# Attention on one core: a full-height second score product, and all key blocks of a unit transposed in one run

## The chip, the cores and the metric

The kernel runs on one core of a Trainium2 chip. Time is device time in microseconds (us) of one execution. Engines are TensorE (PE in the profile, with its weight loads as PEld), VectorE (DVE), ScalarE (ACT), GpSimd (POOL) and SyncE (SP, which issues most transfers). The kernel before takes 1494.95 us, the median of three runs (1494.87 to 1495.86).

## The reference

One post-norm layer of an encoder: 512 tokens, 1024 channels, all in float32. A hybrid mixer (attention in a window and a short gated convolution, both gated and projected) is followed by 16 experts, each of which takes its 64 best tokens. The change touches the attention, which is:

```python
def one_block(args):
    q_blk, n = args
    start = n * BLOCK                       # BLOCK 128, KSPAN 384
    k_blk = lax.dynamic_slice_in_dim(kp, start, KSPAN, axis=1)
    v_blk = lax.dynamic_slice_in_dim(vp, start, KSPAN, axis=1)
    ...
    s = jnp.einsum('bqgrd,bkgd->bgrqk', q_blk, k_blk) + bias
    s = jnp.where(valid, s, NEG_INF)
    m = jnp.maximum(s.max(-1), sink)
    p = jnp.exp(s - m[..., None])
    denom = p.sum(-1) + jnp.exp(sink - m)
    return jnp.einsum('bgrqk,bkgd->bqgrd', p / denom[..., None], v_blk)
```

There are 16 heads of 64 channels in 4 groups (`g`) with one key and value head each, and 4 blocks of 128 queries (`n`). A block of queries sees its own block of keys and its neighbours: three blocks, or two at the ends of the sequence.

## The kernel before

**The mixer's stream.** The mixer's projections are cut into blocks of 128 output columns (`add_blocks`: keys `k`, values `v`, queries `q`, then `c`, `x`, `b` of the convolution, then the gates and output projections). Float32 accuracy comes from splitting both operands into a rounded first part and a rest, in a 32-bit format that TensorE takes in one pass: first x first, first x rest, rest x first, so 3 products of 128x512 for each of 8 slices of the channels. `split_block` makes the parts of the weights: a cast on ScalarE (L165) and a subtraction on VectorE (L166), two blocks ahead. The generator `stream` issues the products (L181); one step of it is one slice, so three products. `F(n)` takes n steps.

**The attention is woven into this stream.** A `Unit` is one group of heads and one block of queries: 4 heads, 2 or 3 key blocks (`w` is 256 or 384 columns). For each unit the code issues 15 steps of the stream and between them the unit's scores for two heads (`scores(0)`), two heads more (`scores(1)`), exponentials (`exps`), the division by the sums (`norms`), and of the unit before it the transposes of the probabilities (`turn`) and the products with the values (`values`). What VectorE, ScalarE and GpSimd do in which order is set by a scheduler that follows program order, with freedom for what is not pinned (`pin`); TensorE keeps the order written here.

**Scores.** `k_done` and `q_done` keep the operands so that one product on 128 rows gives two of the three parts: the keys' first part `kh` lies on both halves of the partitions, and so does the keys' rest `kl`; the queries `qp` hold the first part in one half and the rest in the other. The first product (L480) multiplies the stacked query with `kh` on 128 rows. The second (L481) multiplies the half with the query's first part with `kl` on the same 64 rows. Both add up in one PSUM bank. VectorE then adds the bias and takes the maximum (L484); ScalarE takes the exponentials (L493).

**Transposes and values.** `turn(j)` transposes key block j for 4 heads (L508) into one bank, and ScalarE (j = 0, 2; L513) or VectorE (j = 1; L511) copies it to SBUF. `values` (L520) multiplies it with the values. Scores, transposes and values share a ring of five PSUM banks (`pst`), the stream has three of its own (`mmt`).

**Behind the mixer** the experts' weights (1 MB a load, issued by SP, L603) go through a ring of buffers that the mixer's operands held before; then gate, up and down products of eight pairs of experts follow.

Of the kernel before, what the change touches and what calls it, by code (L numbers as in the profile page):

```python
# [39 lines left out]
def encoder_layer(ctx: ExitStack, tc: tile.TileContext, x, ln0r, ln0c, w_in, conv_w, sink, w_ao, w_co, w_out,  # L40
# [35 lines left out]

# [1 line left out]
    xt = [xpool.tile([P, 2, D], F32, tag=f"X{i}", name=f"x{i}") for i in range(2)]  # L78
# [34 lines left out]
    class Pair:  # L113
        """An operand [P, KT, S] in its two parts, each in two tiles."""

# [14 lines left out]

# [1 line left out]
    loads = []  # L132
# [38 lines left out]
    def stream():  # L171
        opened = {}

        def product(i, k, a, b):
            nm, opnd = blocks[i][2], blocks[i][3]
            if i not in opened:
                opened[i] = ws0.pop(0), mmt(f"p_{nm}")
            ws, ps = opened[i]
            ends = k == KT - 1 and (b if i == 0 else a) == 1
            put = pin if i < 2 else lambda x: x  # L180
            put(nc.tensor.matmul(ps, ws[:, a, k, :], (opnd.lo if b else opnd.hi)(k), start=(k + a + b == 0), stop=ends))  # L181

        def order(i, k):
            """The products of a step: block, index, weight's part, operand's part. Those of the first two blocks fill
            each other's gaps, as their operands are still being made."""
            if i == 0:
                before = [(0, k - 1, 0, 1)] if k else []
                after = [(0, k, 0, 1)] if k == KT - 1 else []
                return [(0, k, 0, 0), (0, k, 1, 0), (1, k, 0, 0)] + before + after
            return ([] if i == 1 else [(i, k, 0, 0)]) + [(i, k, 0, 1), (i, k, 1, 0)]  # L190

        for i, (li, c, nm, opnd, done) in enumerate(blocks):
            for k in range(KT):
                for h in hooks.get((nm, k), ()):
                    h()
                for step in order(i, k):
                    product(*step)
                if k == KT - 1 and i + 2 < len(blocks):
                    ws0.append(split_block(i + 2))
                tick()  # L200
                yield
            done(c, opened.pop(i)[1])
# [10 lines left out]

    # position bias with the window's mask, and the values, by group of heads
    slopes = (2.0 ** (-8.0 * np.arange(1, NH + 1) / NH)).astype(np.float32)
# [10 lines left out]

    # keys: first parts and rests, each on both halves of the partitions; queries: of a head in the upper half of its
    # block the rest lies above the first part, otherwise below
    kh, kl = slot("M0", [NG, S], "kh", F32R), slot("M1", [NG, S], "kl", F32R)
# [103 lines left out]

# [1 line left out]
    src, nm, _ = loads[0]  # L335
# [25 lines left out]
    def root(t):  # L361
        """(var + EPS) ** -0.5 but for the last step, and what that step needs."""
        r, v, a, mean, var = parts0(t)
        pin(nc.scalar.activation(ln[:, t:t + 1], var, AF.Ln, bias=eps))
        pin(nc.scalar.activation(r, ln[:, t:t + 1], AF.Exp, scale=-0.5))
        pin(nc.vector.tensor_scalar(v, var, EPS, -0.5, op0=OP.add, op1=OP.mult))
# [93 lines left out]
    pin(nc.vector.tensor_scalar(sinkb[:, 1, :], sinkb[:, 0, :], -1.0, None, op0=OP.mult))  # L460
# [1 line left out]
    class Unit:  # L462
# [11 lines left out]
        def scores(self, h2):  # L474
            g, w = self.g, self.w
            pss = [pst(f"s_{self.nm}_{i}") for i in range(2)]
            keys = slice(self.b0 * P, self.b1 * P)
            for half in range(2):
                q, hs, ps = qp[g][:, 2 * h2 + half, self.qs], HALVES[half], pss[half][:, :w]
                nc.tensor.matmul(ps, q, kh[:, g, keys], start=True, stop=False)  # L480
                nc.tensor.matmul(ps, q[hs], kl[hs, g, keys], start=False, stop=True)  # L481
            for half in range(2):
                i = 2 * h2 + half
                nc.vector.tensor_tensor_reduce(self.pr[:, i, :w], pss[half][:, :w], bias[g][:, i, self.off:self.off + w],  # L484
                                               1.0, -3.0e38, OP.add, OP.max, self.mx[:, i:i + 1])
# [16 lines left out]

        def turn(self, j):
            if j >= self.b1 - self.b0:
                return
            ps = pst(f"pt_{self.nm}_{j}")
            for i in range(4):
                nc.tensor.transpose(ps[:, i * P:(i + 1) * P], self.pr[:, i, j * P:(j + 1) * P], ident)  # L508
            dst = self.pT[:, j].rearrange("p a b q -> p (a b q)")
            if j == 1:  # L510
                nc.vector.tensor_copy(dst, ps)  # L511
            else:
                nc.scalar.copy(dst, ps)  # L513

# [23 lines left out]
    for g in range(NG):  # L538
        for n in range(NT):
            u = Unit(g, n)  # L540
            u.scores(0)
            F(2)
            u.scores(1)
            F(1)
            u.exps()
            F(1)
            if prev:
                prev.turn(0)
            F(1)
            if prev:  # L550
                prev.turn(1)
            F(1)
            if prev:
                prev.turn(2)
            F(2)
            u.norms()
            F(1)
            if prev:
                prev.values()
            F(6)  # L560
            prev = u
    prev.turn(0)
    F(1)
    prev.turn(1)
    F(1)
    prev.turn(2)
    F(2)
    prev.values()

# [1 line left out]
    wo = {}  # L571
# [64 lines left out]

# [1 line left out]
    aff = const.tile([P, NT, NE], F32, name="aff")  # L638
    # candidates for the largest CAP of each column in two groups of rows: the best of the first two blocks of tokens
    # and most of the third above, the others below; the first two blocks, in two groups; and what is above and at the  # L640
    # bound, behind three empty blocks
    GROUPS, HELD = (slice(0, NE), slice(32, 32 + NE)), CAP // 2 + P
# [13 lines left out]
    def awake(a, n):  # L656
        """Keeps the tensor engine's clock up between products that wait for each other."""
        pin(nc.tensor.matmul(pst("awake")[:a.shape[1], :n], a, xt[0][:, :n], start=True, stop=True))
# [22 lines left out]
    def norm1(t):  # L681
        """Mean and (var + EPS) ** -0.5 of a block, the latter but for the last step; the logits' first part, negated."""
        m, v, l, r = (tinyt(n, f"n1_{a}{t}") for n, a in ((2, "m"), (1, "v"), (1, "l"), (3, "r")))
        st, n = stats[t]
        pin(nc.vector.bn_aggr(m, st[:, :n]))
        pin(nc.scalar.activation(l, m[:, 1:2], AF.Ln, bias=eps))
        pin(nc.scalar.activation(r[:, 0:1], l, AF.Exp, scale=-0.5))
        pin(nc.vector.tensor_scalar(v, m[:, 1:2], EPS, -0.5, op0=OP.add, op1=OP.mult))
        a = tinyt(NE, f"lga{t}")
        pin(nc.vector.scalar_tensor_tensor(a, rc[:, 0, :], m[:, 0:1], lgs[t], op0=OP.mult, op1=OP.subtract))  # L690
        norms1[t] = m, v, r, a
# [45 lines left out]
    def best(src, dst, between=lambda a: None):  # L737
        """The largest CAP of each row of src, in order, into dst; src is used up."""
        for i in range(CAP // 8):
            o = dst[:, 8 * i:8 * i + 8]  # L740
            yield pin(nc.vector.max(o, src))
            if i + 1 < CAP // 8:
                yield pin(nc.vector.match_replace(src, o, src, -1.0))
            between(top[:, 8 * i + 1:8 * i + 9])
# [88 lines left out]

# [1 line left out]
    for i, _ in enumerate(best(cand[:32 + NE], top[:32 + NE, 1:], lambda a: awake(a, 256))):  # L835
# [62 lines left out]
    def spread(ln):  # L898
        """A norm's scale and shift from the first partition to all."""
        def go(i):  # L900
# [19 lines left out]
    def affine():  # L920
        """The scale and shift of the norm, left out so far."""
        for t in range(NT):
# [91 lines left out]

# [1 line left out]
    for t in range(NT):  # L1016
# [88 lines left out]
```

## Time and profile before

| | |
|---|---|
| median of 3 runs without a profile | 1494.95 us |
| span of the profiled execution | 1493.5 us |
| TensorE busy | 1408.8 us, 94% |
| VectorE busy | 402.6 us, 27% |
| ScalarE busy | 292.1 us, 20% |
| share of the chain that ended last: TensorE | 53% |
| share of that chain: transfers | 43% |
| DMA over the span | 451.13 MB, mean 302 GB/s |

The profile comes from one execution of its own; only its span is known, not a time by the clock of the runs. The attention fills the stretch from 55.5 us (first score product) to 308 us (last product with values). Shares over the whole span mix stages with different limits, so what matters for an edit in the attention is read from this stretch. A matmul's recorded duration contains its way through the array and overlaps the next one's; the step from start to start is what a product costs while TensorE has work.

### The profile page before, as it was taken

The page shows a single profiled execution, that of the slowest core. Times are in us where ns is not written, and L with a number is a line of the kernel's source. Part 1 is how long each engine was busy: PE and PEld are TensorE (multiplying, and loading weights), DVE is VectorE, ACT ScalarE, POOL GpSimd, SP SyncE. Part 2 cuts the span into 40 slices and gives each one's busy share as a digit, 9 for nine tenths or more (in the row PEclk, how much of TensorE's full clock was granted, in tenths as well). Part 3 has the DMA queues.
Part 4 walks back from the last instruction along what each step waited for, and adds up shares of the span by engine and source line. Part 5 has one row for each costly group of instructions (what it writes and reads, how often), then busy time and mean ns, then how long its engine had stood idle before and what let it go on. Part 6 is the DMA issues. An engine that isn't in the chain of part 4 may idle for free.

```text
span 1493.5 us, 18062 instructions
## 1 busy us (share of the span) xinstructions
PE 1408.8 (94%) x7559; PEld 808.9 (54%) x7559; DVE 402.6 (27%) x892; ACT 292.1 (20%) x580; POOL 62.1 (4%) x46
## 2 busy tenths in 40 slices
PE   7999999999999999999999998998899799899985
PEld 6777777778888853453553542442452263264243
DVE  8566556653335350010010110010011010011015
ACT  5553444532223221100000000000000000000110
POOL 3000000060000001300000000000000000000001
PEclk9999999999999999999999999999999999999998
DMA  4211113232325969999999999999999999999993
GB/s 150 102 62 57 57 64 106 86 113 85 113 85 198 409 246 356 415 419 419 419 419 420 419 420 419 420 419 420 420 419 420 420 419 418 419 420 419 420 419 155
DMA packets 67205, 451.13 MB, mean 302 GB/s; under 512 B 7730, under 2 KB 10418, under 8 KB 13234
## 3 DMA queue, kind: packets, MB, share of 16 engines
q1 hardware_dynamic: 65824, 446.28, 73.9%
q10 hardware_dynamic: 1300, 3.70, 0.7%
q8 instruction: 59, 0.97, 0.3%
q14 instruction: 22, 0.18, 0.0%
HBM read 447.86 MB, written 2.10 MB: 301 GB/s over the span
## 4 chain that ended last, share of the span: by engine, by line
PE 53%; DMA 43%; DVE 3%; ACT 1%; issue 0%; SPq 0%; DVEq 0%
DMA w<-in_w_gate 25%; DMA w_d<-in_w_down 13%; PE d L983 6%; PE pu L943 4%; PE pg L943 4%; DMA w<-in_w_up 4%; PE p_x L181 3%; PE p_c L181 3%; PE p_b L181 3%; PE p_q L181 3%; PE p_ga L181 3%; PE p_co L181 3%; PE p_ao L181 3%; PE p_gc L181 3%; PE g L879 2%; PE sc L1000 2%
## 5 line engine op out<-in xcount | busy, mean ns | idle before, releaser
L943 PE MATMUL pg<-w,px 128*64 128x512 f32 x1024 | 245.1, 599 | 32.7 <-DMA w<-in_w_gate 32.4
L943 PE MATMUL pu<-w,px 128*64 128x512 f32 x1024 | 246.9, 603 | 16.5 <-DMA w<-in_w_up 16.5
L983 PE MATMUL d<-w_d,hT 128*64 128x256 f32 x2048 | 236.9, 383 | 6.6 <-DMA w_d<-in_w_down 6.5
L983 PEld LDWEIGHTS d<-w_d,hT 128*64 128x64 f32 x2048 | 142.6, 137 | 93.0 <-issue 19.2
L943 PEld LDWEIGHTS pg<-w,px 128*64 128x64 f32 x1024 | 69.0, 136 | 192.8 <-issue 102.2
L943 PEld LDWEIGHTS pu<-w,px 128*64 128x64 f32 x1024 | 64.6, 136 | 146.9 <-issue 96.0
L1005 DVE TENSOR_TENSOR acc<-acc,sc 128x256 f32<-128x256 f32 x108 | 45.5, 421 | 329.0 <-PE sc L1000 328.5
L958 DVE TENSOR_TENSOR h<-h,pu 128x512 f32<-128x512 f32 x32 | 22.0, 687 | 346.2 <-PE pu L943 346.2
L957 ACT ACTIVATE h<-pg 128x512 f32<-128x512 f32 x32 | 19.1, 597 | 331.9 <-PE pg L943 331.9
L1000 PE MATMUL sc<-ye,px 128*128 128x256 f32 x248 | 73.8, 411 | 0.0
L879 PEld LDWEIGHTS g<-px,xn 128*128 128x128 f32 x512 | 59.0, 192 | 20.5 <-issue 17.8
L992 ACT COPY ye<-d 128x256 f32<-128x256 f32 x32 | 11.9, 373 | 275.1 <-PE d L983 275.1
L1000 PEld LDWEIGHTS sc<-ye,px 128*128 128x128 f32 x248 | 40.8, 188 | 43.7 <-issue 41.2
L879 PE MATMUL g<-px,xn 128*128 128x128 f32 x512 | 63.8, 280 | 0.2 <-DVE px L871 0.2
L181 PE MATMUL p_c<-yh,ws_c 128*128 128x512 f32 x128 | 46.6, 411 | 0.0
L181 PE MATMUL p_x<-yh,ws_x 128*128 128x512 f32 x128 | 46.5, 411 | 0.0
L181 PE MATMUL p_b<-yh,ws_b 128*128 128x512 f32 x128 | 46.1, 410 | 0.0
L181 PE MATMUL p_q<-yh,ws_q 128*128 128x512 f32 x128 | 43.6, 403 | 0.0
L493 ACT ACTIVATE pr<-pr,neg 128x256 f32<-128x256 f32 (+1 forms) x64 | 35.2, 552 | 35.1 <-DVE neg L489 24.4
L181 PE MATMUL p_ga<-yh,ws_ga 128*128 128x512 f32 x128 | 40.9, 392 | 0.0
L484 DVE CUSTOM_DVE_ANT_0 pr<-s,bv 128x256 f32<-128x256 f32 (+1 forms) x64 | 31.0, 489 | 33.9 <-PE s L481 33.7
L181 PE MATMUL p_gc<-yh,ws_gc 128*128 128x512 f32 x128 | 40.1, 389 | 0.0
(264 smaller groups left out, 1646.0 us busy)
## 6 DMA issues: line engine op xcount, KB each, us to landing
w<-in_w_gate SPq DMA_DIRECT2D x128, 1024.0 KB, 19.9
w<-in_w_up SPq DMA_DIRECT2D x128, 1024.0 KB, 19.9
w_d<-in_w_down SPq DMA_DIRECT2D x127, 1024.0 KB, 19.9
raw_q<-in_w_in SPq DMA_DIRECT2D x4, 1024.0 KB, 4.8
raw_c<-in_w_in SPq DMA_DIRECT2D x4, 1024.0 KB, 4.8
raw_x<-in_w_in SPq DMA_DIRECT2D x4, 1024.0 KB, 4.9
raw_b<-in_w_in SPq DMA_DIRECT2D x4, 1024.0 KB, 4.8
raw_ga<-in_w_in SPq DMA_DIRECT2D x4, 1024.0 KB, 4.8
```

The source lines that it names most:

```text
L181: put(nc.tensor.matmul(ps, ws[:, a, k, :], (opnd.lo if b else opnd.hi)(k), start=(k + a + b == 0), stop=ends))
L484: nc.vector.tensor_tensor_reduce(self.pr[:, i, :w], pss[half][:, :w], bias[g][:, i, self.off:self.off + w], 1.0, -3.0e38, OP.add, OP.max, ...
L493: nc.scalar.activation(p, p, AF.Exp, bias=self.neg[:, i:i + 1], accum_out=self.su[:, i:i + 1])
L879: pin(nc.tensor.matmul(ps[:, i * P:(i + 1) * P], xt[t][:, (k + i) * P:(k + i + 1) * P], oh1[:, t].rearrange("p a c -> p (a c)"), start=(t ...
L943: pin(nc.tensor.matmul(pss[i][hs, :], xe[:, kk, hs], wt[:, a, k, :], start=(kk == 0), stop=(kk == KT - 1)))
L957: nc.scalar.activation(hb, pss[0], AF.Silu)
L958: nc.vector.tensor_tensor(hb, hb, pss[1], OP.mult)
L983: pin(nc.tensor.matmul(pd[hs, :256], hTs[p][:, f, hs], wt[:, a, ft, :], start=(f == 0), stop=(f == 15)))
L992: nc.scalar.copy(ye, pd[:, :256])
L1000: pin(nc.tensor.matmul(ps[:, :256], ohT[:, t * P:(t + 1) * P], ye, start=True, stop=True))
L1005: nc.vector.tensor_tensor(a, a, ps[:, :256], OP.add)
```

## The change

Two edits, and comments that were taken out (so that lines behind L480 have other numbers in the changed kernel).

1. The second score product takes the whole stacked query and `kl` on all 128 rows. It so adds rest x rest, which was left out before. Both products have the same form.
2. `turn` transposes all key blocks of a unit in one run, into two or three banks, pinned in that order, and then issues the copies. The steps of the stream that lay between the blocks are put around the run; a unit still has 15 steps, and from the second group of scores to the values there are seven as before.

```diff
@@ scores
             for half in range(2):
-                q, hs, ps = qp[g][:, 2 * h2 + half, self.qs], HALVES[half], pss[half][:, :w]
-                nc.tensor.matmul(ps, q, kh[:, g, keys], start=True, stop=False)
-                nc.tensor.matmul(ps, q[hs], kl[hs, g, keys], start=False, stop=True)
+                q, ps = qp[g][:, 2 * h2 + half, self.qs], pss[half][:, :w]
+                for i, k in enumerate((kh, kl)):
+                    nc.tensor.matmul(ps, q, k[:, g, keys], start=(i == 0), stop=(i == 1))
@@ turn
-        def turn(self, j):
-            if j >= self.b1 - self.b0:
-                return
-            ps = pst(f"pt_{self.nm}_{j}")
-            for i in range(4):
-                nc.tensor.transpose(ps[:, i * P:(i + 1) * P], self.pr[:, i, j * P:(j + 1) * P], ident)
-            dst = self.pT[:, j].rearrange("p a b q -> p (a b q)")
-            if j == 1:
-                nc.vector.tensor_copy(dst, ps)
-            else:
-                nc.scalar.copy(dst, ps)
+        def turn(self):
+
+            pss = [pst(f"pt_{self.nm}_{j}") for j in range(self.b1 - self.b0)]
+            for j, ps in enumerate(pss):
+                for i in range(4):
+                    pin(nc.tensor.transpose(ps[:, i * P:(i + 1) * P], self.pr[:, i, j * P:(j + 1) * P], ident))
+            for j, ps in enumerate(pss):
+                dst = self.pT[:, j].rearrange("p a b q -> p (a b q)")
+                if j == 1:
+                    nc.vector.tensor_copy(dst, ps)
+                else:
+                    nc.scalar.copy(dst, ps)
@@ the loop over units
             u.scores(1)
-            F(1)
+            F(2)
             u.exps()
-            F(1)
             if prev:
-                prev.turn(0)
-            F(1)
-            if prev:
-                prev.turn(1)
-            F(1)
-            if prev:
-                prev.turn(2)
+                prev.turn()
+            F(3)
+            u.norms()
             F(2)
-            u.norms()
-            F(1)
             if prev:
                 prev.values()
             F(6)
             prev = u
-    prev.turn(0)
-    F(1)
-    prev.turn(1)
-    F(1)
-    prev.turn(2)
-    F(2)
+    prev.turn()
+    F(4)
     prev.values()
```

TensorE's order where unit 0_1 (group 0, query block 1) is transposed, while unit 0_2 has its scores: `pt_0_1_j` is the bank of key block j, `p_q3_0` a block of the mixer's queries. Before:

```order
L508 MATMUL pt_0_1_0_816<-ident_98,pr_0_1_654 128x128 x4
L181 MATMUL p_q3_0_791<-yh0_278,ws_q3_0_720 128x512
L181 MATMUL p_q3_0_791<-yl0_280,ws_q3_0_720 128x512
L181 MATMUL p_q3_0_791<-yh0_278,ws_q3_0_720 128x512
L508 MATMUL pt_0_1_1_825<-ident_98,pr_0_1_654 128x128 x4
L181 MATMUL p_q3_0_791<-yh1_294,ws_q3_0_720 128x512
L181 MATMUL p_q3_0_791<-yl1_296,ws_q3_0_720 128x512
L181 MATMUL p_q3_0_791<-yh1_294,ws_q3_0_720 128x512
L508 MATMUL pt_0_1_2_834<-ident_98,pr_0_1_654 128x128 x4
```

The same place in the changed kernel:

```order
L508 MATMUL pt_0_1_0_816<-ident_98,pr_0_1_654 128x128 x4
L508 MATMUL pt_0_1_1_817<-ident_98,pr_0_1_654 128x128 x4
L508 MATMUL pt_0_1_2_818<-ident_98,pr_0_1_654 128x128 x4
L181 MATMUL p_q3_0_791<-yh0_278,ws_q3_0_726 128x512
L181 MATMUL p_q3_0_791<-yl0_280,ws_q3_0_726 128x512
L181 MATMUL p_q3_0_791<-yh0_278,ws_q3_0_726 128x512
```

The second and third block's transposes stand one and two steps of the stream earlier.

ScalarE's order at that place, as a difference: `pT_0_1` is the transposed copy of unit 0_1, `pr_0_2` the scores and exponentials of unit 0_2, `q2` and `q3` queries, `ws` parts of weights.

```order
-L513 COPY pT_0_1_655<-pt_0_1_0_816 128x512
+L514 COPY pT_0_1_655<-pt_0_1_0_816 128x512
 L260 ACTIVATE q2_143<-p_q2_1_733 64x512
+L514 COPY pT_0_1_655<-pt_0_1_2_818 128x512
 L493 ACTIVATE pr_0_2_769,su_0_2_766<-pr_0_2_769,neg_0_2_765 128x384 x4
 L494 ACTIVATE es_0_2_767<-es_0_2_767 128x4
-L513 COPY pT_0_1_655<-pt_0_1_2_834 128x512
 L165 CAST ws_c0_0_855<-raw_c0_647 128x1024
```

The third block's copy has moved from behind the four exponentials to ahead of them. In the units 1_0 to 1_3 and 3_0 to 3_3 the copies stand behind the exponentials in both kernels.

VectorE's order at that place, as a difference: `neg_0_2` is the negated maximum that the exponentials read, `es_0_2` the sink's part.

```order
+L512 COPY pT_0_1_655<-pt_0_1_1_817 128x512
+L261 SCALAR_TENSOR_TENSOR q2_143<-p_q2_1_733,q2_143 64x512
 L489 SCALAR_TENSOR_TENSOR neg_0_2_765<-mx_0_2_764,sinkb_94 128x4
 L490 TENSOR_TENSOR es_0_2_767<-sinkb_94,neg_0_2_765 128x4
-L261 SCALAR_TENSOR_TENSOR q2_143<-p_q2_1_733,q2_143 64x512
-L511 COPY pT_0_1_655<-pt_0_1_1_825 128x512
 L497 TENSOR_TENSOR rd_0_2_768<-su_0_2_766,es_0_2_767 128x4
```

The copy of the second block and a query's rest have moved ahead of the negated maximum.

## Rows read from the trace of the kernel before

**Rows 1.** The page: its header, and the granted TensorE clock in 40 slices.
```profile
span 1493.5 us, 18062 instructions
...
PEclk9999999999999999999999999999999999999998
```

**Rows 2.** The chain that ended last: start us, us, engine, what.
```profile
776.50 1.89 PE pu L943 x8
778.41 21.43 DMA w<-in_w_gate
```

**Rows 3.** Windows, the attention: busy us (x instructions) of PE, PEld, DVE, ACT, POOL.
```profile
55.50:308.00 252.50, 252.50 (x1176) 182.29 (x1176) 149.66 (x371) 112.46 (x256) 2.76 (x2) 1.00 0.22 76
```

**Rows 4.** Waits of SP's queue, 400 to 700 us: total, times, longest.
```profile
SPq L603 <- PE pu L943: 53.3, 24, 5.9
```

**Rows 5.** Line L481: duration ns min/median/max, first and last start, forms.
```profile
L481 PE MATMUL s<-kl,q x64: 378/408/439, 55.8 to 291.3; 64*128 64x256 f32 x32, 64*128 64x384 f32 x32
```

**Rows 6.** PE in order of time, two groups of scores: start us, us, what.
```profile
115.89 0.28 PE L480 MATMUL s<-kh,q 128*128 128x256 f32 x1
116.10 0.38 PE L481 MATMUL s<-kl,q 64*128 64x256 f32 x1
116.41 0.38 PE L480 MATMUL s<-kh,q 128*128 128x256 f32 x1
...
117.04 0.50 PE L181 MATMUL p_c<-yh,ws_c 128*128 128x512 f32 x1
117.37 0.39 PE L181 MATMUL p_c<-yl,ws_c 128*128 128x512 f32 x1
117.60 0.63 PE L181 MATMUL p_c<-yh,ws_c 128*128 128x512 f32 x2
...
130.88 0.33 PE L480 MATMUL s<-kh,q 128*128 128x384 f32 x1
131.14 0.43 PE L481 MATMUL s<-kl,q 64*128 64x384 f32 x1
...
132.58 0.39 PE L181 MATMUL p_x<-yl,ws_x 128*128 128x512 f32 x1
```

**Rows 7.** Weight loads in order of time, with idle time and its end.
```profile
115.67 0.19 PEld L480 LDWEIGHTS s<-kh,q 128*128 128x128 f32 x1
116.10 0.18 PEld L481 LDWEIGHTS s<-kl,q 64*128 64x128 f32 x1 [0.24 <-issue]
```

**Rows 8.** PE in order of time, output projection at width 256.
```profile
526.39 0.27 PE L809 MATMUL h<-woh,m 128*128 128x256 f32 x1
526.50 0.28 PE L810 MATMUL h<-wol,m 128*128 128x256 f32 x1
...
527.69 0.29 PE L811 MATMUL h<-woh,m 128*128 128x256 f32 x1
```

**Rows 9.** PE in order of time, transposes of one block and what follows.
```profile
105.36 0.60 PE L508 MATMUL pt<-ident,pr 128*128 128x128 f32 x4
105.71 0.48 PE L181 MATMUL p_c<-yh,ws_c 128*128 128x512 f32 x1
106.02 0.40 PE L181 MATMUL p_c<-yl,ws_c 128*128 128x512 f32 x1
```

**Rows 10.** Groups by form, PE, 55.5 to 308 us: busy us, mean ns | idle.
```profile
L508 PE MATMUL pt<-ident,pr 128*128 128x128 f32 x160 | 23.9, 272 | 0.0
```

**Rows 11.** Waits of the weight loads, 55 to 308 us: total, times, longest.
```profile
PEld p_q L181 <- ACT ws_q L165: 0.2, 1, 0.2
```

**Rows 12.** Groups by form, VectorE, 55.5 to 308 us: busy us, mean ns | idle.
```profile
L484 DVE CUSTOM_DVE_ANT_0 pr<-s,bv 128x384 f32<-128x384 f32 x32 | 17.6, 556 | 15.2 <-PE s L481 15.1
```

**Rows 13.** ACT and PE in order of time: a copy and the values behind it.
```profile
265.09 0.57 ACT L513 COPY pT<-pt 128x512 f32<-128x512 f32 x1
...
266.29 1.08 PE L520 MATMUL o<-pT,bv 128*64 128x256 f32 x8
```

**Rows 14.** PE in order of time: eight transposes of the entry norm.
```profile
11.56 1.09 PE L390 MATMUL ty<-ident,x 128*128 128x128 f32 x8 [1.77 <-ACT x L384]
```

## The prediction

> **What bounds the kernel now.** I read the page's header and slices first. The span is 1493.5 us, and the granted TensorE clock is at the top mark in every slice but the last [rows 1]. The 1494.95 us shown for this kernel are the median of runs without a profile, 1.45 us more than the span; I take these 1.45 us as what lies around the span, and make the sum as a difference to the median.
>
> The chain of waits comes next. In order of time it is TensorE products up to 778 us and weight loads of the experts from there on [rows 2]. So an edit in the attention has to pass two tests: does it shorten TensorE's stream, and does the expert stage start earlier when that stream does.
>
> For the first test, a window over the attention (55.5 to 308 us) shows TensorE busy for all 252.50 us, VectorE for 150 and ScalarE for 112 [rows 3]. A busy mark on TensorE says little, as ends of products are modelled; what counts is the step from one product's start to the next. A product of the mixer (128x512) steps by 0.23 us.
>
> For the second test, the waits of the SP queue from 400 to 700 us tell who holds back the experts' loads: SP waits longest for products that still read the buffers, 53.3 us for the line in front [rows 4]. A buffer ring that TensorE frees is refilled earlier by what TensorE gains. So I take a gain in the attention as passed on 1:1, to the DMA stage as well.
>
> **The second score product.** There are 64 products of each kind, half of them 256 and half 384 columns wide [rows 5], in 32 groups of four (one call of `scores`: keys' first part, keys' rest, and again for the second head).
>
> What a group costs now, in starts: at width 256 the first product starts at 115.89, the second 0.21 us later and the third 0.31 after that; the mixer's next product starts at 117.04, and from it to the one behind it are 0.33 us, where the next step is 0.23 again [rows 6]. From 115.89 to 117.37 are 1.48 us, less 0.23 for the mixer's own product: 1.25 us. At width 384, from 130.88 to 132.58, it is 1.70 - 0.23 = 1.47 us.
>
> Why so much shows in the rows of the weight loads: the load for a product on 64 rows starts 0.43 us after the load before it, and 0.24 us of that pass without a load [rows 7]. It waits for the product on 128 rows to get out of the way. A group changes between 128 and 64 rows four times, and the starts behind the second kind are the late ones.
>
> What it will cost: all four products now use 128 rows of a 32-bit operand of the same kind as the mixer's. The trace has just that form once, at the output projection: 128x256 with its own weight load each time, twelve in a row, starts from 526.39 to 527.69, so 1.30/11 = 0.118 us a step [rows 8]. For 384 columns I take the middle between this and the 0.23 of 512 columns, 0.174 us. Groups then cost 4 x 0.118 = 0.47 and 4 x 0.174 = 0.70 us. They save 0.78 and 0.77 us, over 16 groups each 12.5 + 12.3 = **24.8 us**.
>
> Bounds: the smallest saving that rows allow is with the step that the first product of a group shows today, 0.21 and 0.26 us [rows 6]: 1.25 - 0.84 and 1.47 - 1.04, 16 x (0.41 + 0.43) = 13.4 us. At the other end, the shortest step in the run of 256 is 0.11 [rows 8], 0.5 us more saved in total. I take 0.118: it is the very form, while the 0.21 us has a change of rows right behind it.
>
> A rule here speaks against the edit. The Trainium skill ("TensorE: Matmul & The Clock Gate", Part 3: Packing small matmuls) says that a weight load overlaps running products only where the two use different groups of rows. By it, four products on all rows would pay load and stream one after the other. The trace disagrees: a load for 128 rows is 0.19 us long [rows 7], yet products of that form step by 0.118, each with a load of its own [rows 8]. As a mechanism it is rival 2.
>
> **The transposes in one run.** 160 transposes [rows 10] stay 160. Today they come in 40 runs of four: start to the mixer's next product 0.35 us, and that product takes 0.31 instead of 0.23 [rows 9], 0.43 in all. A run of four spans 0.60 [rows 9] and one transpose lasts 0.27 [rows 10], so the steps inside are (0.60 - 0.27)/3 = 0.11: four cost 0.44 by themselves, and there is no visible price of starting or leaving a run. Joining 40 runs to 16 saves nothing by this; if the 0.08 on the product behind is a price of its own, 24 x 0.08 = 1.9 us. I take 0.
>
> The run moves the last blocks earlier by one or two steps of the mixer, and every unit still has 15 steps. What waits for the copies of the transposed blocks is the product with the values. On ScalarE the copy of the third block used to stand behind the four exponentials and now stands ahead of them in some units (order of unit 0_2); VectorE there copies ahead of the maximum's negation, so the exponentials start later there. Behind them on ScalarE stand a weight cast and nothing that TensorE waits for soon: TensorE's loads waited for such a cast of ScalarE twice in the whole stage, 0.2 us each (one of the two rows stands in [rows 11]). SP's issues keep their order; on ScalarE's queue one reload of the input moves behind such a copy, and its data is first used behind the attention.
>
> One thing is later against the stream. The second score group of a unit now finishes both heads closer together, and the two reductions on VectorE (0.56 us each at width 384 [rows 12]) run one behind the other. So the exponentials, and the copy behind them, come up to 0.5 us later against the products. The closest copy with two blocks ends at 265.09 + 0.57 = 265.66 for a product at 266.29 [rows 13], 0.63 us of room, still enough; with three blocks the last copy is needed only at the fifth product and is itself earlier now. I cost this at nothing; if the cover is gone in the four units where the copy stands behind the exponentials with two blocks, 4 x 0.5 = 2 us.
>
> **Sum.** 1494.95 - 24.8 = **1470.1 us**, the end of the attention 24.8 us earlier and everything behind it moved by the same.
>
> **Rivals.**
> 1. The new products keep the step of today's first one, because two products into one bank with the same queries are limited by something the output projection does not have. For: no run of score products without a change of rows exists in the trace. Against: the output projection also adds up in one bank. 1494.95 - 13.4 = 1481.5.
> 2. Weight load and stream add up (the rule above): 0.19 + 0.118 and 0.19 + 0.174 a step, groups of 1.23 and 1.46 us, 0.5 us saved: 1494.5. Rows 8 speak against it.
> 3. The experts' weight stream sets the end whatever the mixer does. For: loads bound the chain for the last 700 us. Against: the buffers for it come free from TensorE's products [rows 4]. About 1495.
> 4. The clock. A run of twelve transposes is 1.3 us without a product of the mixer. If the clock fell to its lower level (1.2 GHz) during them, all 160 would take twice 0.11: 17.6 us, 1487.7. Against: eight in a run, with 1.77 us of idle time ahead of them [rows 14], lie in a slice at the top mark of the clock [rows 1]. The skill (the same page, Part 4: PE-mode transpose) says that transposes do not count as activity for the clock in the way that products do; by that rule alone this rival would be likelier, but the trace has no stretch that shows it.
> 5. Slower. The run takes three of the five shared PSUM buffers at once, and the second and third of them are those of the unit's first two scores. If VectorE is late with these, TensorE stands in the middle of the run, where before one or two steps of the mixer lay ahead of each. It decides from 24.8/16 = 1.55 us a unit; at 2 us it gives 1502. Against: between the first group and the run lie four steps of three mixer products (12 x 0.23 = 2.8 us) and the second group (0.47), over 3 us for two reductions of at most 0.56.
>
> **How the numbers follow.** Forecast 0.82; rival 1 0.08; rival 2 0.02; rival 3 0.03; rival 4 0.02; rival 5 0.03. Around the forecast: 0.5 us for the step and 1.9 us for the runs below, some 5 us above (2 us at the values' copies and as much again for waits in the other units): 1467.5 to 1476. A range to 1478 reaches towards rival 1 and leaves out 0.18, all the rivals. What a measurement of this kernel tells from no change is 0.2%, 3 us: faster is the forecast with rivals 1 and 4, 0.92; same is rivals 2 and 3, 0.05; slower 0.03.
>
> **What will show it.** In the changed trace the score products have one form, 128 rows, stepping by 0.12 and 0.17 us, and the mixer's product behind a group steps by 0.23. Twelve transposes step by 0.11 throughout. The attention ends near 283 us, the first wait for an expert's weights on the chain lies near 754, and from there nothing changes. I am wrong if the products step by 0.21, if TensorE shows idle time ahead of values or inside a run of transposes, or if the attention is shorter and the span is not.

## The result and the profile after

| | before | after |
|---|---|---|
| median of the runs | 1495.4 us (1494.87 to 1496.09) | 1471.03 us (1470.54 to 1471.87) |
| span of the profiled execution | 1493.5 us | 1469.8 us |
| first score product starts | 55.58 | 56.44 |
| first product of the gates' second block (`p_gc`) starts | 316.39 | 292.66 |
| between these two | 260.81 us | 236.22 us |

The ratio is 0.9838, with a 95% interval from 0.9824 to 0.9852: 24.4 us less, where 24.8 were forecast. The runs of the kernel before in this table are those measured beside the changed kernel; the forecast of 1470.1 us started from 1494.95.

The page of the changed kernel answers to [rows 1]: the span, and the granted clock, which has not moved.

```profile
span 1469.8 us, 18064 instructions
...
PEclk9999999999999999999999999999999999999998
```

The window over the attention (columns as in [rows 3]) shows the same work, but for the last few products, in 228 us instead of 252.5, with TensorE marked busy throughout. VectorE and ScalarE have nearly the same sums as before, so they are denser, and TensorE is still the bound.

```profile
55.50:283.50 228.00, 228.00 (x1181) 181.97 (x1179) 149.22 (x371) 112.72 (x257) 3.51 (x2) 1.00 0.25 85
```

TensorE in order of time, a group of scores at width 256 and one at 384, to be laid beside [rows 6]:

```profile
110.73 0.28 PE L481 MATMUL s<-kh,q 128*128 128x256 f32 x1
110.84 0.28 PE L481 MATMUL s<-kl,q 128*128 128x256 f32 x1
110.96 0.28 PE L481 MATMUL s<-kh,q 128*128 128x256 f32 x1
111.08 0.28 PE L481 MATMUL s<-kl,q 128*128 128x256 f32 x1
111.20 0.40 PE L181 MATMUL p_c<-yh,ws_c 128*128 128x512 f32 x1
111.44 0.40 PE L181 MATMUL p_c<-yl,ws_c 128*128 128x512 f32 x1
...
124.13 0.33 PE L481 MATMUL s<-kh,q 128*128 128x384 f32 x1
124.30 0.34 PE L481 MATMUL s<-kl,q 128*128 128x384 f32 x1
124.47 0.34 PE L481 MATMUL s<-kh,q 128*128 128x384 f32 x1
124.65 0.35 PE L481 MATMUL s<-kl,q 128*128 128x384 f32 x1
124.84 0.40 PE L181 MATMUL p_x<-yh,ws_x 128*128 128x512 f32 x1
```

A group of 256 takes 111.20 - 110.73 = 0.47 us, one of 384 0.71, and the mixer's product behind it steps by 0.24: no price of entering or leaving is left. The forecast had 0.47 and 0.70. Each of the 128 products still has a weight load of its own (line L481: duration in ns as min/median/max, first and last start, form):

```profile
L481 PEld LDWEIGHTS s<-kh,q x64: 186/188/188, 56.2 to 266.9; 128*128 128x128 f32 x64
L481 PEld LDWEIGHTS s<-kl,q x64: 187/188/192, 56.4 to 267.0; 128*128 128x128 f32 x64
```

The transposes of three blocks run as twelve, and some steps of the mixer later the values follow without a wait (TensorE, the mixer's rows left out):

```profile
86.01 1.47 PE L508 MATMUL pt<-ident,pr 128*128 128x128 f32 x12
90.83 1.51 PE L521 MATMUL o<-pT,bv 128*64 128x256 f32 x12
```

At one place TensorE now waits: the last unit's values. The same view, in which each product with the values is recorded twice, so that four rows belong to one key block:

```profile
282.90 0.65 PE L521 MATMUL o<-pT,bv 128*64 128x256 f32 x4
284.46 0.65 PE L521 MATMUL o<-pT,bv 128*64 128x256 f32 x4 [0.90 <-DVE pT L512]
285.04 0.50 PE L181 MATMUL p_ga<-yh,ws_ga 128*128 128x512 f32 x1
```

VectorE there, in order of time, with the same two lines for an earlier piece of work ahead of them:

```profile
273.63 1.22 DVE L166 TENSOR_TENSOR ws_ga<-raw_ga,ws_ga 128x1024 fp32r<-128x1024 f32 x1
274.76 0.69 DVE L291 TENSOR_TENSOR zl<-cc,zh 128x512 fp32r<-128x512 f32 x1
...
279.77 1.22 DVE L166 TENSOR_TENSOR ws_ga<-raw_ga,ws_ga 128x1024 fp32r<-128x1024 f32 x1 [0.39 <-ACT ws_ga L165]
280.91 2.89 DVE L291 TENSOR_TENSOR zl<-cc,zh 128x512 fp32r<-128x512 f32 x1
283.73 0.68 DVE L512 COPY pT<-pt 128x512 f32<-128x512 f32 x1
```

The second block's copy stands behind two subtractions, one of them of 2.89 us, and comes 1.07 us too late: from the first block's values to the second's are 1.56 us, where every other unit has 0.48 or 0.49. In the kernel before, the scheduler put this copy ahead of both, and the slow subtractions came behind it:

```profile
305.77 0.69 DVE L511 COPY pT<-pt 128x512 f32<-128x512 f32 x1 [1.57 <-PE pt L508]
306.38 2.34 DVE L166 TENSOR_TENSOR ws_ga<-raw_ga,ws_ga 128x1024 fp32r<-128x1024 f32 x1
```

For the second test of the forecast, SP's waits from 376 to 676 us repeat [rows 4] to the tenth: what holds the experts' loads back is still the product that reads the buffer.

```profile
SPq L593 <- PE pu L933: 53.3, 24, 5.9
```

One sign was forecast wrongly. The chain that ended last changes from products to loads at 694.85 us, not near 754. From the first product of `p_gc` to the end are 1177.1 us in both kernels, so where the chain changes over did not decide the time.

```profile
693.23 1.62 PE pg L933 x7
694.85 19.90 DMA w_d<-in_w_down
```

### The profile page after: what moved, and what is told of

Its sections match the earlier page's. It is cut to its first block, busy times and chain, and to the rows that moved or that the text cites. A ratio compares the mean times of both kernels' runs of the same rounds, so it can differ in the third digit from the quotient of the medians.

```text
span 1469.8 us, 18064 instructions
## 1 busy us (share of the span) xinstructions
PE 1386.3 (94%) x7559; PEld 810.6 (55%) x7559; DVE 396.8 (27%) x892; ACT 291.8 (20%) x580; POOL 61.8 (4%) x46
## 4 chain that ended last, share of the span: by engine, by line
PE 49%; DMA 47%; DVE 3%; ACT 1%; issue 0%; SPq 0%; DVEq 0%
DMA w<-in_w_gate 26%; DMA w_d<-in_w_down 14%; DMA w<-in_w_up 7%; PE d L973 5%; PE pu L933 4%; PE pg L933 4%; PE p_x L181 3%; PE p_b L181 3%; PE p_c L181 3%; PE p_q L181 3%; PE p_co L181 3%; PE p_ao L181 3%; PE p_gc L181 3%; PE p_ga L181 3%; PE g L869 2%; PE o L521 1%
## 5 line engine op out<-in xcount | busy, mean ns | idle before, releaser
L181 PE MATMUL p_ao<-oh,ws_ao 128*128 128x512 f32 x128 | 40.1, 389 | 0.0
```

## The experiments

Ratios are to runs of the kernel before on the same chip, with their 95% interval. "Attention" is the time from the first score product to the first of `p_gc`, from each profile, 260.81 us in the kernel before.

| run | median us | ratio | attention us |
|---|---|---|---|
| changed kernel | 1471.03 | 0.9838 (0.9824 to 0.9852) | 236.22 |
| scores alone | 1470.44 | 0.9834 (0.9820 to 0.9847) | 236.34 |
| transposes alone | 1497.52 | 1.0012 (1.0003 to 1.0021) | 264.45 |
| two changes a group | 1478.75 | 0.9891 (0.9877 to 0.9904) | 244.81 |
| changed, last copy by ScalarE | 1469.52 | 0.9828 (0.9815 to 0.9841) | 235.15 |
| one score product | 1463.31 | 0.9783 (0.9769 to 0.9798) | 231.52 |
| transposes alone, last copy | 1494.03 | 0.9989 (0.9980 to 0.9998) | 259.61 |
| changed kernel again | 1472.28 | 0.9843 (0.9830 to 0.9857) | 236.23 |
| values whole | 1502.15 | 1.0041 (1.0027 to 1.0055) | 263.54 |
| one score product, last copy | 1460.35 | 0.9767 (0.9753 to 0.9780) | 225.47 |
| changed, last copy, again | 1469.69 | 0.9831 (0.9817 to 0.9844) | 235.16 |

**The scores alone.** The kernel before with the first edit:

```diff
-                q, hs, ps = qp[g][:, 2 * h2 + half, self.qs], HALVES[half], pss[half][:, :w]
-                nc.tensor.matmul(ps, q, kh[:, g, keys], start=True, stop=False)
-                nc.tensor.matmul(ps, q[hs], kl[hs, g, keys], start=False, stop=True)
+                q, ps = qp[g][:, 2 * h2 + half, self.qs], pss[half][:, :w]
+                for i, k in enumerate((kh, kl)):
+                    nc.tensor.matmul(ps, q, k[:, g, keys], start=(i == 0), stop=(i == 1))
```

> The score products of the changed kernel with the transposes of the kernel before, in whose order every engine then works. My theory: all of the gain is here (32 groups of score products, 24.8 us), and the run of transposes costs a wait of about 1.3 us at the last unit's values. Expected 1495.4 - 24.8 = 1470.6, some 1 us under the changed kernel, with score steps of 0.118 and 0.174 us. Rival: the transposes in one run give part of the gain or keep waits away; then this kernel is 2 us or more slower than the changed one, 1473 or above.

Measured 1470.44 us, the attention 24.47 us shorter. That is the forecast of 1470.6. The whole gain is in this edit; the transposes in one run are not needed for it. The steps are those of the changed kernel.

**The transposes alone.** The changed kernel with the score products of the kernel before (the diff above backwards).

> The transposes of the changed kernel in one run, with the score products of the kernel before on 128 and 64 rows. My theory: starting and leaving a run of transposes has no price, so nothing is gained, and the wait for VectorE's last copy (1.3 us) is there: 1495.4 to 1496.7, not faster. Rival: each of the 24 runs that go away saves the 0.08 us that the product behind is late: 1493.5.

Measured 1497.52 us, 1493.41 to 1500.78: slower, by more than I expected, and spread out. TensorE at the last values:

```profile
306.90 0.65 PE L521 MATMUL o<-pT,bv 128*64 128x256 f32 x4
310.62 1.06 PE L521 MATMUL o<-pT,bv 128*64 128x256 f32 x4 [3.07 <-DVE pT L512]
311.61 0.80 PE L181 MATMUL p_ga<-yh,ws_ga 128*128 128x512 f32 x1
312.20 0.63 PE L181 MATMUL p_ga<-yl,ws_ga 128*128 128x512 f32 x1
```

The wait is 3.07 us here, as both subtractions ahead of the copy were slow:

```profile
303.76 3.45 DVE L166 TENSOR_TENSOR ws_ga<-raw_ga,ws_ga 128x1024 fp32r<-128x1024 f32 x1 [0.39 <-ACT ws_ga L165]
307.13 2.83 DVE L291 TENSOR_TENSOR zl<-cc,zh 128x512 fp32r<-128x512 f32 x1
309.88 0.68 DVE L512 COPY pT<-pt 128x512 f32<-128x512 f32 x1
```

And the mixer's first product behind it steps by 0.59 us, where 0.34 is usual behind values and 0.23 further on. Windows of this run (busy columns as in [rows 3], then the granted clock) say why: the clock fell to 0.50 (1.2 GHz) after the wait. It had been 1.00 up to it.

```profile
306.00:310.00 4.00, 1.55 (x9) 0.66 (x7) 4.00 (x3) 1.01 (x1) 4.00 (x3) 1.00 0.46 125
310.00:312.00 2.00, 1.38 (x5) 0.63 (x6) 0.56 (x1) 0.28 (x1) 2.00 (x1) 0.68 0.65 274
312.00:314.00 2.00, 2.00 (x6) 1.52 (x6) 0.42 (x1) 0.09 (x1) 2.00 (x2) 0.50 0.00 0
```

In the changed kernel a wait at the same place stands within a gain of 24 us, which hides it.

**Two changes a group.** The kernel before, in another order:

```diff
             for half in range(2):
+                nc.tensor.matmul(pss[half][:, :w], qp[g][:, 2 * h2 + half, self.qs], kh[:, g, keys], start=True, stop=False)
+            for half in range(2):
                 q, hs, ps = qp[g][:, 2 * h2 + half, self.qs], HALVES[half], pss[half][:, :w]
-                nc.tensor.matmul(ps, q, kh[:, g, keys], start=True, stop=False)
                 nc.tensor.matmul(ps, q[hs], kl[hs, g, keys], start=False, stop=True)
```

> The kernel before, with the four products of a group in another order: both on 128 rows first, then both on 64 rows (one on the lower, one on the upper half). A group then changes between 128 and 64 rows twice instead of four times. My theory (the price is in the changes): 0.12 between the first two, 0.21 into the 64 rows, 0.31 + 0.10 out of them, between the two on 64 rows anything from 0 (at once, in two halves of the array) to 0.12: 0.74 to 0.86 us a group of width 256 instead of 1.25, 12 to 16 us saved over 32 groups: 1479 to 1483. Rival (a product on 64 rows is slow by itself): no saving, 1495.

Measured 1478.75 us, 16.5 us less than before and just past the better end of the forecast (1479 to 1483). The rival, no saving, is out. A group of 256 in order of time; the two products on 64 rows, in different halves, have run together (x2 in 0.38 us, the length of one):

```profile
112.66 0.40 PE L479 MATMUL s<-kh,q 128*128 128x256 f32 x2
112.99 0.38 PE L482 MATMUL s<-kl,q 64*128 64x256 f32 x2
113.30 0.50 PE L181 MATMUL p_c<-yh,ws_c 128*128 128x512 f32 x1
113.64 0.40 PE L181 MATMUL p_c<-yl,ws_c 128*128 128x512 f32 x1
```

The group takes 113.64 - 112.66 - 0.23 = 0.75 us, against 1.25 before and 0.47 after: even with the second pair for the price of one, a way into the 64 rows and out again costs more than the full height.

This run changed two things: the changes between 128 and 64 rows were halved, and the two products on 64 rows ran at once. What a change costs is seen in the products of 128 rows beside them. The one ahead steps by 0.21 us into 64 rows [rows 6], where it steps by 0.12 into another of its own form. The mixer's one behind steps by 0.34 (113.64 - 113.30) instead of 0.23. These 0.2 us are about half of the 0.39 that each second product costs over the full height ((1.25 - 0.47) / 2). The other half is in the 0.31 us from a product on 64 rows to the next, and here it stays open whether the way out takes it or the product itself: no run has two such products on the same rows one behind the other.

**The last copy by ScalarE.** The changed kernel, with one more condition, set for the last unit alone:

```diff
...
-                if j == 1:
+                if j == 1 and not last:
                     nc.vector.tensor_copy(dst, ps)
...
```

> The changed kernel, with the last unit's second block copied by ScalarE instead of VectorE, so that it isn't queued behind the slow subtraction of 2.9 us. My theory: the 1.3 us that TensorE waited at the last values go, and the end moves with it: 1471.0 - 1.3 = 1469.7. Rival: the wait is given back at the next place (the entry norm on ScalarE runs 0.6 us later, and VectorE's weight parts stay late) and the time stays at 1471.

Measured 1469.52 us, and 1469.69 in the repetition below; the last values run through without a wait, although the subtractions are as slow as ever (3.16 and 2.86 us):

```profile
282.44 1.08 PE L521 MATMUL o<-pT,bv 128*64 128x256 f32 x8
```

The wait was worth its 1.07 us in the attention (236.22 to 235.15). This version is under both kernels: its eight runs, with the repetition, lie between 1469.05 and 1470.34 us, the nine of the changed kernel between 1470.54 and 1474.29.

**One score product.**

```diff
-                for i, k in enumerate((kh, kl)):
-                    nc.tensor.matmul(ps, q, k[:, g, keys], start=(i == 0), stop=(i == 1))
+                nc.tensor.matmul(ps, q, kh[:, g, keys], start=True, stop=True)
```

> The changed kernel without the second score product: the term of the queries with the keys' rest is left out of the scores. My theory: a product costs its step and the end of the kernel moves with the attention 1:1, so 64 products fewer save 32 x 0.118 + 32 x 0.174 = 9.3 us on the changed kernel: 1461.7. Rival: the experts' weight stream or another engine takes part of what the attention gains from here on; then the time is 1465 or above.

Measured 1463.31 us (1460.3 to 1466.49), between the two expectations. By itself this would have spoken for the rival. The profile shows that it doesn't: TensorE waited 3.10 us for the last copy, and the granted clock behind it (the third figure from the end of the window) was 0.50.

```profile
276.54 1.12 PE L520 MATMUL o<-pT,bv 128*64 128x256 f32 x4 [3.10 <-DVE pT L511]
...
277.00:279.00 2.00, 2.00 (x7) 1.17 (x4) 0.42 (x1) 0.37 (x1) 2.00 (x2) 0.50 0.22 86
```

The run without that wait is the one that decides:

> The changed kernel with ScalarE's last copy and without the second score product: the term of the queries with the keys' rest is left out of the scores. Without the wait at the last values, which hid the result of the same edit before. My theory: 1:1, 9.3 us under the kernel with ScalarE's last copy alone, 1460.2. Rival: the later stages take part of it: 1463 or above.

Measured 1460.35 us. Against 1469.69 of the same kernel with both products, measured beside it, that is 9.3 us, the forecast to the tenth: 32 steps of 0.118 and 32 of 0.174 us, passed on to the end. The attention got 9.69 shorter (235.16 to 225.47). Over all twelve profiles the stretch from the first product of `p_gc` to the end takes between 1176.3 and 1177.9 us, with an attention between 225.5 and 264.5: what the attention gains or loses is passed on 1:1, to within these 1.6 us.

**The transposes alone, with the last copy by ScalarE.** Both small diffs together.

> Only the transposes in one run, with the scores of the kernel before and the last unit's second block copied by ScalarE, so that the wait at the last values, 3.2 us in the run with this edit alone, is away. My theory: the run of transposes has no price and no gain: 1495.3, within 0.5 us of the kernel before. Rival: the 24 runs of transposes that go away are worth 0.08 us each: 1493.4.

Measured 1494.03 us, between the two, and a little under the kernel before (ratio 0.9989, 0.9980 to 0.9998); the attention is 1.20 us shorter. The edit has a gain, then, that the wait hid: with the wait of 3.07 us and the low clock behind it the attention had been 4.84 us longer than here (264.45). The starts of the values' products say where it is. First the kernel before, then this run:

```profile
219.34 1.51 PE L520 MATMUL o<-pT,bv 128*64 128x256 f32 x12
235.16 1.08 PE L520 MATMUL o<-pT,bv 128*64 128x256 f32 x8
236.83 0.65 PE L520 MATMUL o<-pT,bv 128*64 128x256 f32 x4
250.89 1.08 PE L520 MATMUL o<-pT,bv 128*64 128x256 f32 x8
```

```profile
219.84 1.52 PE L521 MATMUL o<-pT,bv 128*64 128x256 f32 x12
235.62 1.52 PE L521 MATMUL o<-pT,bv 128*64 128x256 f32 x12
250.97 1.08 PE L521 MATMUL o<-pT,bv 128*64 128x256 f32 x8
```

In two of the 16 units of the kernel before (at 235.16, and again at 297.98) the scheduler lets two products of the mixer between the values' products, and they step into and out of the form on 64 columns once more. From one unit's values to the next are 15.73 us there and 15.35 in this run; the unit ahead, which wasn't split, has 15.82 and 15.78.

**Values whole.** The kernel before with all of TensorE's mixer, score, transpose and values' products pinned, and the last copy by ScalarE:

```diff
-            put = pin if i < 2 else lambda x: x
+            put = pin
...
-                nc.tensor.matmul(ps, q, kh[:, g, keys], start=True, stop=False)
-                nc.tensor.matmul(ps, q[hs], kl[hs, g, keys], start=False, stop=True)
+                pin(nc.tensor.matmul(ps, q, kh[:, g, keys], start=True, stop=False))
+                pin(nc.tensor.matmul(ps, q[hs], kl[hs, g, keys], start=False, stop=True))
... (the transposes and the values' products pinned in the same way, and the copy)
```

> The kernel before, transposes in three runs, but with TensorE held to the written order, so that no values' products of a unit are split by two products of the mixer (the scheduler does that in units 2_2 and 3_2 of the kernel before), and with the last unit's second block copied by ScalarE. My theory now: the 1.2 us that the transposes in one run gained, with the wait taken away, come mostly from these two splits, each an extra change into and out of the values' products on 64 columns (0.25 us by the rows of before): attention from the first score to the first product of gc 260.3 to 260.0 us, time 0.5 to 0.8 us under the kernel before. Rival: they come from the 24 runs of transposes that went away; then the attention stays at 260.8 us.

As a time it failed: 1502.15 us, 7 us slower. Held to the written order, TensorE waits early in the stream, before the units in question: 3.12 us at the transposes of the values at 42 us, with the granted clock at 0.50 behind it, so that the first score product starts at 62.36 instead of 55.58 us; and 0.26 and 1.34 us more within the first unit's scores, after which the clock fell again (0.63 from 68 to 70 us).

```profile
42.14 1.12 PE L248 MATMUL vt<-ident,vs 128*128 128x128 f32 x4 [3.12 <-ACT vs L243]
...
44.00:46.00 2.00, 2.00 (x6) 1.56 (x5) 0.05 (x1) 0.00 (x0) 0.00 (x0) 0.50 0.00 0
```

The units themselves can still be read, as nothing waits there:

```profile
229.56 1.52 PE L520 MATMUL o<-pT,bv 128*64 128x256 f32 x12
245.38 1.52 PE L520 MATMUL o<-pT,bv 128*64 128x256 f32 x12
260.76 1.08 PE L520 MATMUL o<-pT,bv 128*64 128x256 f32 x8
```

The unit that was split takes 15.38 us instead of 15.73: 0.35 us a split where 0.25 were expected, 0.7 for the two, without the transposes joined. From there to the 15.35 of the run with joined transposes, and from 15.82 to 15.78 in the unit ahead, 0.03 to 0.04 us a unit are left for the joining, some 0.5 us over 16 units. So of the 1.2 us about 0.7 come from the splits and the rest from the runs: neither the theory nor the rival has it alone, and the time that was forecast stays untested.

**The two repetitions.**

> The changed kernel once more, beside the others of this call: 1471.0, and a wait of about 1 us ahead of the last unit's second block of values. If that wait varies with the length of the slow subtraction on VectorE in front of it, the time varies by as much from run to run.

The median was 1472.28, 1.3 us above the expectation, and the runs spread from 1470.64 to 1474.29; the profiled one has the wait as before, 0.90 us of idle time.

> The changed kernel with ScalarE's last copy, once more beside the two others of this call: 1469.5, no wait at the last values, and no run above 1470.5. If it is the wait that makes the changed kernel's runs spread (1470.6 to 1474.3), these spread by less than 1 us.

1469.69 us, 1469.21 to 1470.34: a spread of 1.1 us, a little over the 1 us expected, against 3.7. That fits the late copy as the cause of the spread; the wait of the unprofiled runs can't be seen, so this is inferred.

The profiles suggest what makes the wait long or short. In the four with VectorE's late copy, the first of the two subtractions starts just ahead of GpSimd's first multiplication of the entry norm in two (279.77 against 279.99 in the changed kernel, 279.11 against 279.16 in its repetition): it takes 1.22 us, and TensorE waits 0.90. In the other two it starts just behind it (303.76 against 303.72 in the transposes alone, 269.66 against 269.65 in the run with one product): it takes 3.45 and 3.48 us, and TensorE waits 3.07 and 3.10. So less than 0.3 us in the start of either engine goes with 2.2 us of wait. No run moved GpSimd's work by itself, so this is read from the profiles and not tried.

## Why the prediction was right

**The score products** were the term, and it held in size: 0.47 and 0.71 us a group against 0.47 and 0.70, 24.47 us of attention in the run with this edit alone against 24.8. The choice of the step from the output projection over that from today's first product was the point that decided; the latter's 13.4 us are excluded by every run with this edit. That changes of rows were the price, and not the 64 rows, was an argument then. The run with two changes a group and the steps of the products beside show it for about half of the price; for the other half it stays an argument.

**1:1 to the end.** Shown in both directions: the gain of the attention passes the expert stage in full, and 9.3 us more of it in the run without the second product.

**The transposes in one run** were costed at 0, with 1.9 us as the bound. Without the wait they gain 1.2 us. The forecast missed that TensorE's own order had two split units: rows of the trace show them (235.16 and 236.83 above), and my account of the kernel said that TensorE keeps the written order, which is not so in these two units. Nor is it so in the second score group of the first unit, which is split in both kernels (at 59.13 and 61.14 us in the kernel before); that group saves 0.62 us and not 0.78.

**No wait at the values** is the step that failed, by 1.07 us. I watched ScalarE's copy behind the exponentials; its room with two blocks went from 0.63 us to 0.58 (copy to 244.43, product at 245.01) and no product waited for it. The copy that came late is VectorE's in the last unit, behind two subtractions that the new order put ahead of it. I had followed VectorE's order only at a unit's own instructions, and not at the end of the attention.

**The sum** was partly luck: 24.47 + 1.20 - 1.07 = 24.60 us, and the attention got 24.59 shorter. The gain and the wait that the forecast both had at nothing nearly cancel, so the sum came out better than its terms.

**The rivals.** Rival 1 (steps of 0.21) and rival 2 (load and stream add up) are excluded by steps of 0.118 between products that each have a load of their own. The rule behind rival 2 (the Trainium skill, "TensorE: Matmul & The Clock Gate", Part 3: Packing small matmuls) does not hold here. Rival 3 is excluded by the 1:1. Rival 4: the granted clock was 1.00 through all the attention of the changed kernel, with its runs of twelve transposes; where it fell, in the three runs above with waits of 3 us, TensorE had stood idle just before. In the attention no run has a longer stretch of transposes without a product between them. Rival 5: no transposes waited for a buffer.

## What to carry to other kernels

Half of the array's rows is no saving when it stands among products of full height: look at the steps into and out of such a product, and fill the rows up with whatever adds nothing harmful. Price a form that is not in the stage by the same form elsewhere in the trace, and not by its nearest neighbour in a disturbed sequence. After an edit that moves instructions, read the changed order of each engine at the ends of the loop too, behind what a copy that TensorE needs is queued, and not only in the steady state.

## What was not expected of the hardware

- A product on 64 rows among products on 128 makes a group of four cost 0.78 us more at 256 columns (1.25 against 0.47); two on different halves of the rows run at the same time.
- Waits of TensorE of 3.07 and 3.10 us were followed by a granted clock of 0.50 for the next products, which made them cost more than themselves: 4.84 and 6.05 us of attention against the same kernels without the wait (264.45 to 259.61, 231.52 to 225.47). Waits of 0.90 us left the clock at 1.00.
- VectorE's subtraction of 128x512 (L291) took 0.68 or 0.69 us in the 84 cases of all profiles in which GpSimd stood idle, and 2.83 to 2.89 in the 12 in which it was multiplying. The one of 128x1024 (L166) took 1.21 to 1.23 us in the 746 without GpSimd's work, and 1.22 to 3.48 in the 46 that met it. The copy of 128x512 from PSUM took 0.68 us even then (283.73 in the changed kernel). That GpSimd's work is the cause was not tried by moving it alone.
